# A rounded copy traced ahead of the squares, a tile in another pool, and another pacing of background loads, in a one-core encoder block

## The chip, the cores and the metric

The kernel runs on one core of one Trainium2 chip. The metric is the device time of one execution in microseconds (us). The kernel before took 1969.74 us (median of 3 runs, 1966.11 to 1972.82).

## What is computed

One encoder block on a single sequence of T = 256 tokens of width D = 2048, all in fp32. Two branches read the same normalised input, are merged by gates, and a feed-forward layer follows.

```python
mod = c_act @ ada_w + ada_b                 # six vectors of 2048: shift, scale, gate (mixer), shift, scale, gate (FFN)
h = rms_norm(x, norm_mix_w) * (1 + scale_m) + shift_m
proj = h @ w_in                             # all inputs of both branches and the merge gates
...
h_a = bidirectional(mlstm_chunkwise, ...)   # branch A: 4 mLSTM heads, key width 256, value width 512
y_a = (sigmoid(a_o) * rms_norm(h_a)) @ w_branch_a
...
q_b = l2_normalize(heads(b_q, B_HEADS, B_DK)) * (B_DK ** -0.5)
k_b = l2_normalize(heads(b_k, B_HEADS, B_DK))
o_b = bidirectional(gated_delta_chunkwise, ...)  # branch B: 16 delta-rule heads of width 128
y_b = (rms_norm(o_b) * silu(b_z)) @ w_branch_b
...
x = x + gate_m * ((g_a * y_a + g_b * y_b) @ w_out)
hf = rms_norm(x, norm_ffn_w) * (1 + scale_f) + shift_f
x = x + gate_f * ((silu(gt) * up) @ w_down) # gt, up = split(hf @ w_gate_up), width 5632
```

The result is a final RMSNorm of `x`.

## The kernel before, in words

**Weight jobs.** Nearly all of PE's time goes to products with weights. A weight block of 1 MB (`raw_...`, three buffers) is loaded by SP's queue. It is split in halves: ACT writes the rounded copy `wh_...` (L207 or L176), DVE the rest `wl_...` = raw minus copy (L209 or L178), and PE multiplies `wh` by the high part of the activations, `wh` by the low part, and `wl` by the high part. A half of a block is one step of a job, and `wh` and `wl` have three buffers each. `tjob` and `fjob` are these jobs (`fjob` for operands that come out transposed). The weight of a job is in its name: `b` and `a` for the input projection of the delta branch and of the mLSTM queries and keys, `z`, `v`, `o`, `mb`, `ma` for gates and values, `yb` and `ya` for the output projections of the branches B and A, `o` again for `w_out`, then `gt`, `up` and `d` for the feed-forward layer.

**Order.** The program is traced once in the order in which Python generators yield: `fill(n)` takes n steps of the jobs in `fills`, `drive(cores, n)` alternates a step of the branch work with n steps of jobs, and `settle()` traces evictions that were put off. A scheduler of the language then lays out one queue for each engine. It starts from the traced order and moves an instruction whose inputs or buffer it expects late behind others; an instruction that is passed through `order()` keeps its place in the program's order. On the chip each engine works through its own queue in that order and waits on semaphores, so that whatever stands behind a waiting instruction on its engine waits with it. A change of buffers alone can therefore move instructions.

**Delta heads.** For each of the 16 heads `gdn_phase1` has `kq` (queries and keys, 128x512) in fp32. ACT makes the squares `sqkq` (L596), whose sums PE takes with a column of ones (`vps`, L605) for the normalisation, and the rounded copy `kqh` (L599); DVE makes the rest `kql` (L600), and PE multiplies the split parts. `sqkq`, `kqh` and `kql` have one buffer each. At the end of a pair of heads PE transposes the result into `px` (L835), ACT scales it into `obt` (L839, 128x256, two buffers in the pool `bk`), and ACT's queue stores it to the DRAM tensor `ob_d` (L840). Group g of four heads is one tensor `ob_d[g]`.

**From branch B to its output projection.** When all heads are done, `sx.close()` gives up `bk` and the pools beside it; `ml`, which holds what the mLSTM heads need (`dn`, `hs`, `o4` and others), takes that memory. Then `o_load(g)` reads `ob_d[g]` into `o4` (L1070, GpSimd's queue, two buffers), and `o_split` makes `obh` (ACT, L1074) and `obl` (DVE, L1075), the operands of the `yb` jobs. In the same stretch the first two mLSTM heads finish: `pden` (PE, L956) are the denominators, `dn` (ACT, L958) their absolute values, `ph` (PE, L972) the numerators, `hs` (L974, L975) the quotient. `pxa` (L988) are its transposes, `hah` and `hal` (L992, L993) its split.

**The eviction pool.** `evp` lies on the other side of memory and lives until `sa.close()`. `keep_f` evicts the `a` jobs through its two buffers of tag `evf` (L355 to L357, stored to `kq_d`).

**Background loads.** The vectors of `mod` need `ada_w`: 64 blocks of 1 MB in parts of 16, each loaded into `ada` (L114, SP's queue) and multiplied and summed on DVE (L122, one instruction of 128x2048). `pump()` runs once for each step of a job. It lets an `add()` through at most once in `every[0]` steps, and not before the load is three steps old; only one block is asked for at a time, from the pool `rows_p`. `held` stops the adds for a while.

Of the kernel before, what the change touches and what calls it, by code (L numbers as in the profile page):

```python
# [9 lines left out]
F32 = mybir.dt.float32  # L10
F32R = mybir.dt.float32r
AF = mybir.ActivationFunctionType
# [3 lines left out]
P = 128  # L16
T = 256
D = 2048
# [34 lines left out]
def hybrid_block(ctx: ExitStack, tc: tile.TileContext, xr, nfr, crow, pk_d, cst_d, ada2, ada4, win0, winb, wint, wba, wbb, wo, wgu, wd, out, dbg=None):  # L53
    nc = tc.nc
    V, S, G, PE = nc.vector, nc.scalar, nc.gpsimd, nc.tensor

    def pool(stack, name, bufs=1, **kw):
        return stack.enter_context(tc.tile_pool(name=name, bufs=bufs, **kw))
# [3 lines left out]
    rows_p = pool(ctx, "rows")  # L62
# [9 lines left out]
    def order(ins, yes=True):  # L72

        return tc.keep_in_program_order(ins) if yes else ins

    def gps(name):
        return g_ps.tile([P, 512], F32, tag="g", name=name)
# [27 lines left out]
        order(S.activation(row_c[:, g * 512 : (g + 1) * 512], pc_, AF.Silu))  # L105


    asked, unasked, age = [], [], [0]

    def ask():  # L110

        part, b = unasked.pop(0)
        raw = rows_p.tile([P, D], F32, tag="ada", name=f"ada{part}_{b}")
        order(nc.sync.dma_start(raw, ada4[part - 2, b]))  # L114
        asked.append((part, b, raw))
        age[0] = 0

    def add():

        part, b, raw = asked.pop(0)  # L120
        c = part * KB + b
        order(V.scalar_tensor_tensor(raw, raw, 1.0, row_c[:, :D], ALU.mult, ALU.mult, accum_out=mod[:, c : c + 1]))  # L122
        if b == KB - 1:
            c = slice(part * KB, part * KB + KB)
            V.tensor_tensor(mod[:, c], mod[:, c], pk[:, PK_ADAB + c.start : PK_ADAB + c.stop], ALU.add)
# [18 lines left out]
    count, every = [0], [0]  # L144
    owed, held = [0], [False]

    def sums(n=1):

        while n and (unasked or asked):
            if not asked:  # L150
                ask()
            add()
            n -= 1

    def pump():
        count[0] += 1
        age[0] += 1
        if every[0] and count[0] % every[0] == 0:
            owed[0] = 1
        if asked:  # L160
            if owed[0] and age[0] > 2 and not held[0]:
                owed[0] = 0
                add()
        elif unasked and every[0]:
            ask()

    def fjob(name, src, done):

        ps = acc_ps.tile([P, 512], F32, tag="acc", name=f"acc_{name}")
        o = ps[:, :T]  # L170
        raw = raw_tile([P, KB, P], f"raw_{name}")
        nc.sync.dma_start(raw, src)
        for k0 in range(0, KB, 8):
            wh = st.tile([P, 8, P], F32R, tag="wh", bufs=3, name=f"wh_{name}_{k0}")
            wl = st.tile([P, 8, P], F32R, tag="wl", bufs=3, name=f"wl_{name}_{k0}")
            S.activation(wh, raw[:, k0 : k0 + 8], AF.Copy)  # L176
            settle()
            V.tensor_tensor(wl, raw[:, k0 : k0 + 8], wh.bitcast(F32), ALU.subtract)  # L178
            for k in range(8):
                kk = k0 + k  # L180
                PE.matmul(o, wh[:, k], woven(hh[:, kk]), start=kk == 0, stop=False)  # L181
                PE.matmul(o, wh[:, k], woven(hl[:, kk]), start=False, stop=False)  # L182
                PE.matmul(o, wl[:, k], woven(hh[:, kk]), start=False, stop=kk == KB - 1)  # L183
            pump()
            if k0:
                done(o.rearrange("p (c h) -> p h c", h=2))
            yield True
# [5 lines left out]
    def tjob(name, chunks, xh, xl, done, early=0, by_token=None, steps=1, parts=((0, slice(0, 512)), (1, slice(0, 512)))):  # L193
# [28 lines left out]
        for n, (u, k0) in enumerate(todo):  # L222
            wh, wl = made.pop(0) if made else halves(u, k0)
            for k in range(2):
                kk = 4 * u + k0 + k
                for t in range(2):
                    c = slice(t * P, (t + 1) * P)
                    order(PE.matmul(ps[t], xh[:, kk, c], woven(wh[:, k]), start=kk == 0, stop=False), early and steps > 1)  # L228
                    PE.matmul(ps[t], xl[:, kk, c], woven(wh[:, k]), start=False, stop=False)  # L229
                    PE.matmul(ps[t], xh[:, kk, c], woven(wl[:, k]), start=False, stop=kk == last)  # L230
            pump()
            if k0:
                if u == len(chunks) - 1:
                    done(ps)
            yield True
            if early and steps > 1:
                if n + early < len(todo):
                    made.append(halves(*todo[n + early]))
                yield True
# [23 lines left out]
    def fill(n=1):  # L263

        while n and fills:
            if next(fills[0], None):
                n -= 1
            else:
                fills.pop(0)
# [23 lines left out]
    evp = pool(sa, "evp", side="right")  # L293
    fr = pool(sf, "fr", side="right")
# [192 lines left out]
    with ExitStack() as s0:  # L487
# [18 lines left out]
        def loads(b):  # L506
            ra = [w0.tile([P, D + 2], F32, tag="ra", bufs=5, name=f"ra{b}_{i}") for i in range(2)]
            raw = st.tile([P, N0, P], F32, tag="raw", bufs=3, name=f"raw0_{b}")
            for i in range(2):
                order(nc.sync.dma_start(ra[i], ada2[b, :, i]))  # L510
            order(nc.sync.dma_start(raw, win0[b]))
            return ra, raw
# [10 lines left out]
        ra, raw = loads(0)  # L523
# [18 lines left out]
        for b in range(KB):  # L542
            if b:
                ra, raw = loads(b)
# [23 lines left out]
    bk = pool(sx, "bk")  # L568
# [12 lines left out]
    def gdn_phase1(h):  # L581
        settle()
        kq, vf = parts.pop(h)
# [8 lines left out]
            dec[:, 1, 256:384][:, ::-1], ab[:, 0:P][:, ::-1], ident[:, ::-1], 0.0, ALU.mult, ALU.add  # L592
        )

        sq = fr.tile([P, 2, T], F32, tag="sqkq", bufs=1, name=f"sqkq{h}")
        S.activation(sq, kq, AF.Square)  # L596
        kh = fr.tile([P, 2, T], F32R, tag="kqh", bufs=1, name=f"kqh{h}")
        kl = fr.tile([P, 2, T], F32R, tag="kql", bufs=1, name=f"kql{h}")
        S.activation(kh, kq, AF.Copy)  # L599
        V.tensor_tensor(kl, kq, kh.bitcast(F32), ALU.subtract)  # L600
        vps = gps(f"vps{h}")
        for t in range(2):
            PE.transpose(vps[:, t * P : (t + 1) * P], vf[:, t * P : (t + 1) * P], ident)
# [139 lines left out]
    def gdn_phase2(g, p):  # L743
# [88 lines left out]
        for e, on in enumerate(ons):  # L832
            h, hl_ = 4 * g + 2 * p + e, 2 * p + e
            for t in range(2):
                PE.transpose(px[:, (2 * e + t) * P : (2 * e + t + 1) * P], on[:, t], ident)  # L835
        for e in range(2):
            h, hl_ = 4 * g + 2 * p + e, 2 * p + e
            obt = bk.tile([P, T], F32, tag="obt", bufs=2, name=f"obt{h}")
            S.activation(obt, px[:, e * T : (e + 1) * T], AF.Copy, scale=pk[:, PK_GNW + h : PK_GNW + h + 1])  # L839
            S.dma_start(ob_d[g][hl_], obt)  # L840
        yield
# [27 lines left out]
    def steps(*gens):  # L869

        gens = list(gens)
        while gens:
            gens = [g for g in gens if next(g, "end") != "end"]
            if gens:
                yield

    def drive(gen, n=2):
        for _ in gen:
            fill(n)
# [29 lines left out]
    def mlstm(h):  # L909
# [84 lines left out]
        yield  # L994

    heads1 = {h: gdn_phase1(h) for h in range(NH_B)}
    after = (0, 1, 2, 1, 2, 2, 2, 2, 4, 0)
    last = (0, 1, 2, 1, 2, 2, 1, 1, 3, 0)
# [21 lines left out]
    for g in range(4):  # L1020
# [3 lines left out]
        next(blocks)  # L1024
        fill(1)
        pairs = [gdn_phase2(g, p) for p in range(2)]
        if g == 3:
            settle()
# [39 lines left out]
    def o_load(g):  # L1068
        o4 = ml.tile([P, 4, T], F32, tag="o4", bufs=2, name=f"o4_{g}")
        G.dma_start(o4, ob_d[g].rearrange("h p t -> p h t"))  # L1070
        return o4
# [40 lines left out]
            yield from y_b(g)  # L1112

    o4s = [o_load(g) for g in range(2)]
    held[0] = False
    cores = steps(*first2)
    fill(1)
# [20 lines left out]
    o_split(3, o4s[3])  # L1138
    fill(2)
    drive(cores, 3)  # L1140
    drive(steps(mlstm(2), mlstm(3)), 3)
    fill(1000)
    mgh, mgl = big(bigC, F32R, "mgh"), big(bigC, F32R, "mgl")
    sm_.close()
    sr_ = ExitStack()
    sr = pool(sr_, "sr")
    gm = sr.tile([P, D], F32, name="gm")
    dgs = {}

# [31 lines left out]
    def o_job(g, front=None):  # L1181
        return tjob(f"o{g}", [wo[g, u] for u in range(4)], mgh, mgl, lambda *a: done_o(g, *a), by_token=front,
                    parts=((0, slice(0, 512)), (1, slice(0, 256)), (1, slice(256, 512))))
# [24 lines left out]
    def root():  # L1208

        order(S.activation(rs1[:, 2:3], ones1, AF.Sqrt))  # L1210
# [83 lines left out]
    for g in range(4):  # L1294
        if g == 3:
            root()
        for i, _ in enumerate(o_job(g, front_o if g == 3 else None) if g else o_first, 0 if g else 2):
            if g == 3 and i == 3:
                every[0] = owed[0] = 0
                sums(P)  # L1300
                V.scalar_tensor_tensor(
                    affn, mod[:, 4 * KB : 5 * KB], 1.0, pk[:, PK_NFFN : PK_NFFN + KB], ALU.add, ALU.mult
                )
# [78 lines left out]
    for j in range(FB // 4):  # L1382
# [4 lines left out]
        for e2 in range(2):  # L1387
            px = gps(f"pxf{j}_{e2}")
            for e in range(2):
                f = 2 * e2 + e  # L1390
                for t in range(2):
                    PE.transpose(px[:, e * T + t * P : e * T + (t + 1) * P], sg[:, t, f * P : (f + 1) * P], ident)  # L1392
            b = 4 * j + 2 * e2
# [156 lines left out]
```

## Time and profile before

| | |
|---|---|
| median of 3 runs | 1969.74 us |
| the profiled execution | 1972.23 us |
| its span in the trace | 1970.2 us |
| mean granted TensorE clock | 0.996 |
| PE busy | 1926.1 us (98%) |
| DVE busy | 1405.9 us (71%) |
| ACT busy | 1028.4 us (52%) |
| POOL busy | 116.5 us (6%) |
| moved by DMA | 485.64 MB, mean 246 GB/s |

PE, DVE, ACT and POOL are TensorE, VectorE, ScalarE and GpSimd; PEld is TensorE's weight load, and ACTq the queue of DMAs that ACT issues. The span starts with the first and ends with the last instruction in the trace; the profiled time is 2.0 us longer. In rows of the timeline the columns are the start, the duration in us, the engine, the line, the operation, output<-input and the count; in brackets stand the idle time of the engine before it and what ended it.

### The profile page before, as it was taken

To read this page: it belongs to the slowest core of one execution; us is meant where nothing else is said; L and a number is where in the kernel's file an instruction comes from. 1 tells how busy PE (TensorE), PEld (TensorE's weight loads), DVE (VectorE), ACT (ScalarE), POOL (GpSimd) and SP (SyncE) were. 2 spreads that over 40 slices of the span, in tenths; PEclk is the share of its full clock that TensorE was granted. 3 is DMA by queue.
4 is the path that set the end of the run, shared out by engine and by line. 5 is a ranking of instruction groups with operands and counts; after the bars stand their busy time and mean duration, and the time that the engine had idled before them with its cause. 6 is when DMAs were issued, how large, how long until landed. Compare 5 with 4: busy or idle time off the path is not lost. (4 is left out here: it accounts for less than half of the span.)

```text
span 1970.2 us, 27078 instructions
## 1 busy us (share of the span) xinstructions
PE 1926.1 (98%) x10418; PEld 1701.1 (86%) x10418; DVE 1405.9 (71%) x2067; ACT 1028.4 (52%) x1553; POOL 116.5 (6%) x211
## 2 busy tenths in 40 slices
PE   8999999999999999999899999999999999999998
PEld 6878889998999899889687888888888888888886
DVE  6779886888888789866577877865665665555554
ACT  3137656765776587554534444644444444444444
POOL 0001210111011101010100000200000000000000
PEclk9999999999999999999999999999999999999999
DMA  9986676667676666587786888576676665565553
GB/s 400 421 348 225 186 248 253 206 227 232 221 226 205 225 217 237 201 287 250 268 321 220 314 314 321 213 256 235 241 269 238 235 241 206 194 214 199 207 200 142
DMA packets 78962, 485.64 MB, mean 246 GB/s; under 512 B 10585, under 2 KB 15969, under 8 KB 24433
## 3 DMA queue, kind: packets, MB, share of 16 engines
q1 hardware_dynamic: 63216, 450.69, 62.9%
q0 software_dynamic: 8160, 17.88, 4.4%
q10 hardware_dynamic: 7458, 15.36, 2.0%
q8 instruction: 81, 1.33, 0.3%
q14 instruction: 47, 0.39, 0.1%
HBM read 467.07 MB, written 16.82 MB: 246 GB/s over the span
## 5 line engine op out<-in xcount | busy, mean ns | idle before, releaser
L209 DVE TENSOR_TENSOR wl_d<-raw_d,wh_d 128x1024 fp32r<-128x1024 f32 x88 | 107.7, 1225 | 105.9 <-ACT wh_d L207 105.9
L209 DVE TENSOR_TENSOR wl_up<-raw_up,wh_up 128x1024 fp32r<-128x1024 f32 x88 | 107.7, 1225 | 100.2 <-ACT wh_up L207 100.1
L209 DVE TENSOR_TENSOR wl_gt<-raw_gt,wh_gt 128x1024 fp32r<-128x1024 f32 x88 | 108.1, 1229 | 79.2 <-ACT wh_gt L207 79.2
L181 PE MATMUL acc_b<-hh,wh_b 128*128 128x256 f32 x576 | 162.9, 283 | 0.0
L183 PE MATMUL acc_b<-hh,wl_b 128*128 128x256 f32 x576 | 159.2, 277 | 0.1
L182 PE MATMUL acc_b<-hl,wh_b 128*128 128x256 f32 x576 | 159.1, 276 | 0.0
L207 ACT ACTIVATE wh_d<-raw_d 128x1024 fp32r<-128x1024 f32 x88 | 92.9, 1056 | 126.4 <-PE acc_d L229 117.6
L207 ACT ACTIVATE wh_gt<-raw_gt 128x1024 fp32r<-128x1024 f32 x88 | 92.9, 1055 | 118.6 <-PE acc_gt L229 71.1
L122 DVE SCALAR_TENSOR_TENSOR ada<-ada,crow 128x2048 f32<-128x2048 f32 x64 | 146.2, 2284 | 7.1 <-DMA ada<-ada 7.1
L207 ACT ACTIVATE wh_up<-raw_up 128x1024 fp32r<-128x1024 f32 x88 | 92.8, 1055 | 108.1 <-PE acc_up L229 77.1
L228 PE MATMUL acc_gt<-wh_gt,hfh 128*128 128x512 f32 x352 | 135.5, 385 | 0.6 <-ACT hfh L1337 0.6
L229 PE MATMUL acc_gt<-wh_gt,hfl 128*128 128x512 f32 x352 | 135.1, 384 | 0.0
L230 PE MATMUL acc_gt<-wl_gt,hfh 128*128 128x512 f32 x352 | 133.9, 380 | 0.0
L228 PE MATMUL acc_up<-wh_up,hfh 128*128 128x512 f32 x352 | 133.4, 379 | 0.0
L229 PE MATMUL acc_up<-wh_up,hfl 128*128 128x512 f32 x352 | 133.4, 379 | 0.0
L230 PE MATMUL acc_up<-wl_up,hfh 128*128 128x512 f32 x352 | 133.4, 379 | 0.0
L228 PE MATMUL acc_d<-wh_d,ffh 128*128 128x512 f32 x344 | 130.5, 379 | 0.0
L229 PE MATMUL acc_d<-wh_d,ffl 128*128 128x512 f32 x344 | 130.5, 379 | 0.0
L230 PE MATMUL acc_d<-wl_d,ffh 128*128 128x512 f32 x344 | 130.4, 379 | 0.0
L555 PE MATMUL first<-x,raw 128*128 128x256 f32 x512 | 114.5, 382 | 6.6 <-ACT x L549 6.2
L555 PEld LDWEIGHTS first<-x,raw 128*128 128x128 f32 x512 | 96.0, 190 | 25.0 <-ACT x L549 11.9
L181 PEld LDWEIGHTS acc_b<-hh,wh_b 128*128 128x128 f32 x576 | 111.4, 193 | 0.1
(383 smaller groups left out, 5257.8 us busy)
## 6 DMA issues: line engine op xcount, KB each, us to landing
ada<-ada SPq DMA_DIRECT2D x64, 1024.0 KB, 6.2
raw_gt<-wgu SPq DMA_DIRECT2D x44, 1024.0 KB, 4.9
raw_up<-wgu SPq DMA_DIRECT2D x44, 1024.0 KB, 4.9
raw_d<-wd SPq DMA_DIRECT2D x44, 1024.0 KB, 4.9
raw_b<-winb SPq DMA_DIRECT2D x36, 1024.0 KB, 5.6
ra<-ada SPq DMA_DIRECT2D x32, 1025.0 KB, 15.7
raw<-win SPq DMA_DIRECT2D x16, 1024.0 KB, 14.5
raw_z<-wint SPq DMA_DIRECT2D x16, 1024.0 KB, 5.2
```

What stands on the lines that cost most here:

```text
L122: order(V.scalar_tensor_tensor(raw, raw, 1.0, row_c[:, :D], ALU.mult, ALU.mult, accum_out=mod[:, c : c + 1]))
L181: PE.matmul(o, wh[:, k], woven(hh[:, kk]), start=kk == 0, stop=False)
L182: PE.matmul(o, wh[:, k], woven(hl[:, kk]), start=False, stop=False)
L183: PE.matmul(o, wl[:, k], woven(hh[:, kk]), start=False, stop=kk == KB - 1)
L207: order(S.activation(wh, raws[u][:, k0 : k0 + 2], AF.Copy), early)
L209: order(V.tensor_tensor(wl, raws[u][:, k0 : k0 + 2], wh.bitcast(F32), ALU.subtract), early)
L228: order(PE.matmul(ps[t], xh[:, kk, c], woven(wh[:, k]), start=kk == 0, stop=False), early and steps > 1)
L229: PE.matmul(ps[t], xl[:, kk, c], woven(wh[:, k]), start=False, stop=False)
L230: PE.matmul(ps[t], xh[:, kk, c], woven(wl[:, k]), start=False, stop=kk == last)
L555: PE.matmul(first[o], raw[:, o], x[:, b], start=b == 0 and o % 2 == 0, stop=b == KB - 1 and o % 2 == 1)
```

## The change

It has three parts.

1. In `gdn_phase1` the rounded copy `kqh` and the rest `kql` are traced ahead of the squares `sqkq`.
2. The tile `obt` is taken from `evp` under the tag `evf`, instead of from `bk` under a tag of its own. The two buffers are then shared with the evictions of the `a` jobs.
3. The pacing of the `ada` loads. A list `homes` holds the buffers that are free to be loaded into: one in `rows_p`, and from the opening of the pool `sr` on, ahead of the `ya` jobs, a second one there. Each load carries its own age, and a load is asked for in the same `pump()` as an add, from the home that was free before it. `every[0]` is set to 0 after the first two `o_load`s, to 1 ahead of the third and fourth mLSTM heads, and to 3 when `sr` has opened. In the last `o` job, `sr`'s home is taken out again.

```diff
-    asked, unasked, age = [], [], [0]
+    asked, unasked, homes = [], [], [rows_p]
...
-        raw = rows_p.tile([P, D], F32, tag="ada", name=f"ada{part}_{b}")
+        home = homes.pop(0)
+        raw = home.tile([P, D], F32, tag="ada", name=f"ada{part}_{b}")
         order(nc.sync.dma_start(raw, ada4[part - 2, b]))
-        asked.append((part, b, raw))
-        age[0] = 0
+        asked.append([part, b, raw, home, 0])
...
-        part, b, raw = asked.pop(0)
+        part, b, raw, home, _ = asked.pop(0)
+        homes.append(home)
...
     def pump():
         count[0] += 1
-        age[0] += 1
+        for a in asked:
+            a[-1] += 1
         if every[0] and count[0] % every[0] == 0:
             owed[0] = 1
-        if asked:
-            if owed[0] and age[0] > 2 and not held[0]:
-                owed[0] = 0
-                add()
-        elif unasked and every[0]:
+        more = bool(unasked and every[0] and homes)
+        if asked and owed[0] and asked[0][-1] > 2 and not held[0]:
+            owed[0] = 0
+            add()
+        if more:
             ask()
...
-        sq = fr.tile([P, 2, T], F32, tag="sqkq", bufs=1, name=f"sqkq{h}")
-        S.activation(sq, kq, AF.Square)
         kh = fr.tile([P, 2, T], F32R, tag="kqh", bufs=1, name=f"kqh{h}")
         kl = fr.tile([P, 2, T], F32R, tag="kql", bufs=1, name=f"kql{h}")
         S.activation(kh, kq, AF.Copy)
         V.tensor_tensor(kl, kq, kh.bitcast(F32), ALU.subtract)
+        sq = fr.tile([P, 2, T], F32, tag="sqkq", bufs=1, name=f"sqkq{h}")
+        S.activation(sq, kq, AF.Square)
...
-            obt = bk.tile([P, T], F32, tag="obt", bufs=2, name=f"obt{h}")
+            obt = evp.tile([P, T], F32, tag="evf", bufs=2, name=f"obt{h}")
...
     o4s = [o_load(g) for g in range(2)]
+    every[0] = owed[0] = 0
     held[0] = False
...
     drive(cores, 3)
+    every[0] = 1
     drive(steps(mlstm(2), mlstm(3)), 3)
...
     sr = pool(sr_, "sr")
+    homes.append(sr)
+    every[0] = 3
...
                 every[0] = owed[0] = 0
                 sums(P)
+                homes.remove(sr)
```

The lines shift by 1 to 7: L207 becomes L209, L839 L841, L958 L960, L1074 L1076.

ACT's queue at the handover from branch B to the `yb` jobs, before. `obt_9347` and `obt_9350` are the last two heads' results, `dn_9382` and `dn_9399` the denominators of the first two mLSTM heads, `wh_yb_1_0` the rounded copy of the second weight block of the first `yb` job; a wait on DMAHW or DMASW is one on a DMA's landing.

```order
L349 ACTIVATE ev_ma_9339<-acc_ma_1_9137 128x512 [waits PE_49]
L839 ACTIVATE obt_9347<-px_1_9257,pk 128x256 [waits PE_49]
L350 DMA ma_d_115<-ev_ma_9339 128x1024 [waits Activation_49]
L840 DMA ob_d_123<-obt_9347 128x256 [waits DMAHW7_49,Activation_49]
L839 ACTIVATE obt_9350<-px_1_9257,pk 128x256
L207 ACTIVATE wh_yb_1_0_9510<-raw_yb_1_9508 128x1024 [waits DMAHW2_49]
L840 DMA ob_d_123<-obt_9350 128x256 [waits Activation_49]
L958 ACTIVATE dn_9382<-pden_9375 128x4 [waits DMASW5_49,DMASW6_49,DMASW4_49,DMAHW0_49,DMASW3_49,DMAHW7_49,DVE_49,PE_49]
L958 ACTIVATE dn_9399<-pden_9392 128x4 [waits PE_49]
L974 ACTIVATE hs_9387<-ph_0_0_9411,dn_9382 128x512 [waits DVE_49,PE_49]
```

The same place now:

```order
L841 ACTIVATE obt_9347<-px_1_9257,pk 128x256 [waits DMAHW4_49,PE_49]
L352 DMA ma_d_115<-ev_ma_9339 128x1024 [waits DMAHW5_49,Activation_49]
L842 DMA ob_d_123<-obt_9347 128x256 [waits DMAHW7_49,Activation_49]
L841 ACTIVATE obt_9350<-px_1_9257,pk 128x256
L960 ACTIVATE dn_9382<-pden_9375 128x4 [waits DMASW4_49,DMASW5_49,DMASW3_49,DMASW6_49,DVE_49,PE_49]
L960 ACTIVATE dn_9399<-pden_9392 128x4 [waits PE_49]
L842 DMA ob_d_123<-obt_9350 128x256 [waits DMAHW1_49,Activation_49]
L1076 ACTIVATE obh<-o_0_9369 128x1024 [waits DMASW3_49]
L976 ACTIVATE hs_9387<-ph_0_0_9411,dn_9382 128x512 [waits DVE_49,PE_49]
L209 ACTIVATE wh_yb_1_0_9508<-raw_yb_1_9506 128x1024 [waits DMAHW2_49]
```

The waits DMAHW7 and DMAHW0 at the first `dn` are gone (the landings of the two stores of `obt`, whose memory `dn` took over), `dn` stands ahead of the second store, and `obh` of group 0 stands ahead of `hs` instead of three instructions behind it. The first `obt` has a new wait (DMAHW4, the landing of an earlier store of an `a` job's eviction).

DVE's queue in the first `yb` job, before. `obl` from `o_2` and `o_3` are the low parts of groups 2 and 3, `ada_8` a background add, `wl_yb_u_k` the low part of half k of weight block u.

```order
L1075 TENSOR_TENSOR obl<-o_2_9409,obh 128x1024 [waits DMASW7_49,Activation_49]
L209 TENSOR_TENSOR wl_yb_1_2_9529<-raw_yb_1_9508,wh_yb_1_2_9528 128x1024 [waits PE_49,Activation_49]
L1075 TENSOR_TENSOR obl<-o_3_9429,obh 128x1024 [waits DMASW0_49,Activation_49]
L122 SCALAR_TENSOR_TENSOR ada_8_9490,mod<-ada_8_9490,crow 128x2048 [waits DMAHW4_49]
L209 TENSOR_TENSOR wl_yb_2_0_9548<-raw_yb_2_9545,wh_yb_2_0_9547 128x1024 [waits DMAHW3_49,PE_49,Activation_49]
```

The same place now:

```order
L1077 TENSOR_TENSOR obl<-o_2_9409,obh 128x1024 [waits DMASW7_49,Activation_49]
L1077 TENSOR_TENSOR obl<-o_3_9429,obh 128x1024 [waits DMASW0_49,Activation_49]
L211 TENSOR_TENSOR wl_yb_1_2_9527<-raw_yb_1_9506,wh_yb_1_2_9526 128x1024 [waits PE_49,Activation_49]
L211 TENSOR_TENSOR wl_yb_2_0_9545<-raw_yb_2_9542,wh_yb_2_0_9544 128x1024 [waits DMAHW3_49,PE_49,Activation_49]
L981 RECIPROCAL ssh_9406<-ssh_9406 128x2 [waits Activation_49]
```

The add of `ada_8` has left this place (and that of `ada_9`, which stood between the first and the second `yb` job); `ada_8` now stands ahead of the last half of the second `yb` job. `wl_yb_1_2` has moved behind `obl` of group 3. From the `ya` jobs on the adds stand every third step; before, every fourth. PE's queue has the same order but for some 20 instructions, and GpSimd's is unchanged.

In a delta head ACT's queue shows the first part of the change. Before, for the fifth head:

```order
L335 ACTIVATE kq_2481<-cv_1_2566 128x256 [waits DVE_49]
L596 ACTIVATE sqkq_2739<-kq_2481 128x512 [waits Activation_49]
L327 ACTIVATE pad_144<-acc_b_2_2583 128x256 [waits PE_49]
L599 ACTIVATE kqh_2741<-kq_2481 128x512
L330 ACTIVATE cv_2_2647<-pad_144,pk 128x256 [waits Activation_49]
```

And now:

```order
L337 ACTIVATE kq_2481<-cv_1_2566 128x256 [waits DVE_49]
L599 ACTIVATE kqh_2739<-kq_2481 128x512 [waits Activation_49]
L329 ACTIVATE pad_144<-acc_b_2_2583 128x256 [waits PE_49]
L602 ACTIVATE sqkq_2743<-kq_2481 128x512
L332 ACTIVATE cv_2_2647<-pad_144,pk 128x256 [waits Activation_49]
```

The two have changed places, with one eviction of a weight job (`pad`) between them; in the second and the fourth head the squares stay in front, where `kqh` has to wait for its single buffer.

## The prediction, made before the changed kernel was run

> **What bounds the kernel now.** The page's first part comes first.
>
> ```profile
> PE 1926.1 (98%) x10418; PEld 1701.1 (86%) x10418; DVE 1405.9 (71%) x2067; ACT 1028.4 (52%) x1553; POOL 116.5 (6%) x211
> ```
>
> PE sets the time: of 1970.2 us it is idle for 44, and none of its matmuls is removed here. So the change is worth what it takes from PE's waits or adds to them. The windows view tells where it waits.
>
> ```profile
> 0.00:150.00 150.00, 138.75 (x602) 113.90 (x603) 103.53 (x124) 42.09 (x78) 2.26 (x10) 1.00 0.95 385
> ...
> 955.00:1010.00 55.00, 46.48 (x200) 34.70 (x201) 36.83 (x50) 27.14 (x43) 9.33 (x15) 1.00 0.89 321
> ...
> 1080.00:1165.00 85.00, 85.00 (x408) 74.61 (x407) 71.34 (x75) 39.80 (x42) 0.00 (x0) 1.00 0.82 305
> ```
>
> The columns are the length, PE's busy time, then PEld, DVE, ACT and POOL, the granted clock, the DMA engines' busy share and GB/s. Between 955 and 1010 us, the handover to the `yb` jobs, PE idles 8.5 of 55 us; in the `ya` stage (1080 to 1165) it idles for nothing. The waits view of PE for 955:1010 names three rows, which sum to 8.5 us:
>
> ```profile
> PE acc_yb L230 <- DVE wl_yb L209: 3.5, 3, 1.6
> PE ph L972 <- ACT dn L958: 2.7, 1, 2.7
> PE pxa L988 <- DVE hal L993: 2.3, 1, 2.3
> ```
>
> All three lie where the second and third part of the change act. The timelines of the engines show why each arises.
>
> **The tile `obt` in another pool: the wait at `dn`.** The first two rows are ACT's, then two of PE's; the last row is from the view of `obt`'s tile.
>
> ```profile
> 955.66 0.33 ACTq L840 DMA_DIRECT2D ob_d<-obt  x1
> 961.69 0.24 ACT L958 ACTIVATE dn<-pden 128x4 f32<-128x4 f32 x2 [5.12 <-DMA ob_d<-obt]
> 956.40 2.82 PE L972 MATMUL ph<-vt,mdec 128*128 128x512 f32 x6
> 961.92 7.99 PE L972 MATMUL ph<-vt,mdec 128*128 128x512 f32 x18 [2.70 <-ACT dn L958]
> DMA to landing us min/median/max: 1.8/3.0/6.5
> ```
>
> `dn` takes over the memory of `obt`, so it waits until the last store of `obt` has landed, about 6 us after its issue; PE's next `ph` needs the bank that `dn` empties, and PE idles 2.70 us. With `obt` in the other pool this wait is gone from `dn`. Next in line for PE is `hs`, which in ACT's new order stands behind `obh` of group 0, and that on the load of `o_0`:
>
> ```profile
> 953.37 0.60 PE L835 MATMUL px<-cst,on 128*128 128x128 f32 x4
> 962.21 1.51 POOL L1070 DMA_DIRECT2D o<-ob_d  x2 [61.30 <-ACT dn L958]
> 967.79 1.06 ACT L1074 ACTIVATE obh<-o 128x1024 fp32r<-128x1024 f32 x1 [3.10 <-DMA o<-ob_d]
> 970.16 0.19 PEld L229 LDWEIGHTS acc_yb<-wh_yb,obl 128*128 128x128 f32 x1 [0.65 <-DVE obl L1075]
> DMA to landing us min/median/max: 4.5/5.3/6.3
> ```
>
> The last row is the view of line 1070. The load of `o_0` waited for the same stores of `obt`, and is free of them now: its memory is free after the `px` transposes of the first row, at 954.0. It lands 5.3 us later, at 959.3; `obh` takes 1.06 and `hs`, half its size, an estimated 0.7, so `hs` is out at about 961.1. PE runs through twelve `ph` passes of 0.44 (7.99 / 18) from 956.40 to 961.7 before it needs that bank. So the whole 2.70 us goes, with half a microsecond to spare; if the load takes its longest, 6.3, half a microsecond of wait is left. `obl` of group 0 is done by 963, ahead of the first `yb` matmul at 967: the 0.65 us of the fourth row goes too. **Gain 2.7 + 0.6 = 3.3.**
>
> The Trainium skill speaks against the 2.7 (DMA: Bandwidth & Descriptors, "Anatomy of one DMA"): a transfer costs about 2.0 us fixed plus its bytes at 436 GB/s. By that, a 128 KB store lands in an estimated 2.3 us, `dn` would have been in time, and the gain here would be near 0; the page adds that a landing in HBM can be surprisingly late, and the measured wait decides.
>
> **The first `yb` job: three waits for `wl`.** Rows of ACT, DVE and PE:
>
> ```profile
> 976.46 1.04 ACT L207 ACTIVATE wh_yb<-raw_yb 128x1024 fp32r<-128x1024 f32 x1
> 977.41 1.04 ACT L1074 ACTIVATE obh<-o 128x1024 fp32r<-128x1024 f32 x1
> 977.73 1.22 DVE L209 TENSOR_TENSOR wl_yb<-raw_yb,wh_yb 128x1024 fp32r<-128x1024 f32 x1
> 980.00 2.28 DVE L122 SCALAR_TENSOR_TENSOR ada<-ada,crow 128x2048 f32<-128x2048 f32 x1
> 982.21 1.22 DVE L209 TENSOR_TENSOR wl_yb<-raw_yb,wh_yb 128x1024 fp32r<-128x1024 f32 x1
> 979.00 0.48 PE L230 MATMUL acc_yb<-wl_yb,obh 128*128 128x512 f32 x1 [0.59 <-DVE wl_yb L209]
> 983.48 0.48 PE L230 MATMUL acc_yb<-wl_yb,obh 128*128 128x512 f32 x1 [1.62 <-DVE wl_yb L209]
> ```
>
> The fifth half block waits 1.62 us because DVE did an add of 2.28 us ahead of its `wl`. That add has left this place. The fourth waits 0.59 since its split stood between the two late `o` loads, and this gets no better: it now stands behind `obh` of `o_3`. `o_3` takes the buffer of `o_1`; ACT has five instructions between `hs` and `obh` of `o_1`, so that I put `obl` of `o_1` at 967.6 (an estimate). `o_3` is issued then, lands 5.3 later at 972.9, `obh`, `wh` and `wl` follow (1.06 + 1.04 + 1.22) at about 976.4, while PE, which starts the job at 967.0 (956.40 + 24 x 0.44) and takes 2.6 us a half, wants `wl` at about 975.2. I put the fourth half's wait at 1.2 us, 0.6 more than before. **Gain 1.6 - 0.6 = 1.0**; between 0 (`o_3` a microsecond later) and 2.2 (both waits gone).
>
> **The second `yb` job: an add that waits for its load.**
>
> ```profile
> 992.77 2.29 DVE L122 SCALAR_TENSOR_TENSOR ada<-ada,crow 128x2048 f32<-128x2048 f32 x1 [4.55 <-DMA ada<-ada]
> 999.59 2.87 DVE L993 SCALAR_TENSOR_TENSOR hal<-pxa,pk,hah 128x256 fp32r<-128x256 f32 x7
> 996.77 1.55 ACT L992 ACTIVATE hah<-pxa,pk 128x256 fp32r<-128x256 f32 x4
> 996.27 0.48 PE L230 MATMUL acc_yb<-wl_yb,obh 128*128 128x512 f32 x1 [1.28 <-DVE wl_yb L209]
> 1000.13 0.44 PE L988 MATMUL pxa<-cst,hs 128*128 128x128 f32 x2 [2.30 <-DVE hal L993]
> ```
>
> DVE stood for 4.55 us on the load of the next add and then added for 2.29; queued behind it were the `wl` that PE waits 1.28 us for and the `hal` that `pxa` waits 2.30 for. With neither load nor add in this stretch, `wl` is in time (1.3 gone). `hal` then follows `hah`, which ACT starts at 996.77 behind a weight copy; four of them would let `hal` end about 1.7 us earlier, and some 0.6 us of the wait stay. **Gain 1.3 + 1.7 = 3.0**; 1.3 if `hah` is no earlier at all, 3.6 if ACT's copy moves up too.
>
> **The heads.** The waits view has one row for the squares, and head 4's timeline the distance:
>
> ```profile
> PE vps L605 <- ACT sqkq L596: 0.3, 1, 0.3
> 340.04 0.62 ACT L599 ACTIVATE kqh<-kq 128x512 fp32r<-128x512 f32 x1
> 345.19 0.95 PE L605 MATMUL vps<-ones,sqkq 128*128 128x1 f32 x8
> ```
>
> Squares in the place of `kqh` end at 340.66, 4.5 us ahead of the sums that need them; no wait on `kqh` or `kql` is among PE's. The 0.3 us may grow by one activation (0.62) or go. **0**, from -0.3 to +0.6. What hides it is PE's weight jobs between; without them each of the 16 heads would pay 0.6.
>
> **What it costs.** `obt` now waits for the landing of an eviction's store in the shared buffers (view of line 357, and ACT at one of these places):
>
> ```profile
> DMA to landing us min/median/max: 1.7/4.1/7.7
> 740.52 0.84 ACT L839 ACTIVATE obt<-px,pk 128x256 f32<-128x256 f32 x2 [0.41 <-PE px L835]
> ```
>
> Where an `a` job's store is issued a step before, ACT stands 1 to 3 us by the 4.1, an estimated four times in all; the weight copies behind it are a step (2.6 us) ahead of PE. **Cost 0.3**, between 0 and 4 (1 us each). The denser adds in `ya` and `o`: 408 matmuls in 85 us are 17 blocks of 24, so a block takes 5.0 us and a step 2.5. An add of 2.28 us every 7.5 us in place of every 10 takes DVE from 71.34 of 85 us (84%) to about 91%. **Cost 0.5**, from 0 to the rival below.
>
> A last term is the clock. The windows view of 1029:1034:
>
> ```profile
> 1029.00:1034.00 5.00, 5.00 (x17) 4.10 (x16) 2.60 (x6) 1.02 (x2) 0.00 (x0) 0.66 0.78 261
> ```
>
> A granted clock of 0.66 over 5 us is 3.4 us at half speed, which costs PE 1.7 us; it comes behind a burst of one-column matmuls. Such a spell may come or go when the work ahead of it moves by microseconds: 0, +-1.7. The Trainium skill (TensorE: Matmul & The Clock Gate, "What's actually happening") has a free-running window of 3413 ns, which fits the length; by its rule the halving follows an idle window, and here PE had just been busy.
>
> **Sum:** 3.3 + 1.0 + 3.0 - 0.3 - 0.5 = 6.5 us less. The profiled execution took 1972.23 us (its span 1970.2), 2.5 over the median of the runs; 1972.23 would become 1965.7, and by the same step the median of 1969.74 becomes **1963.2 us**.
>
> **The rivals.**
>
> *All of it goes.* If `hah` moves up and the fourth half's split is in time, the three rows fall from 8.5 to nothing, and with `obl`'s 0.65 and a clock spell less the gain is 9 to 11: about 1960. For it: nothing but loads sets these times, and two 1 MB loads leave a stretch where the DMA engines are 0.89 busy. Against: the `o_3` chain above.
>
> *Another wait takes the place of `dn`'s.* The store's landing at 6.5 us is the longest of 16, the median is 3.0. If it was short in the timed runs, the 2.7 was never there; or the `o_0` load is late, and `hs` behind `obh` holds PE in its place. Either way 3.3 goes and 3 to 4 is left: about 1966.5.
>
> *Slower: the loads crowd out the weights.* From the `ya` jobs on, a load of 1 MB comes every 7.5 us in place of every 10: the 305 GB/s would become about 340. These rows are landings of 1 MB:
>
> ```profile
> raw<-win SPq DMA_DIRECT2D x16, 1024.0 KB, 14.5
> raw_ya<-wba SPq DMA_DIRECT2D x16, 1024.0 KB, 5.6
> ```
>
> The first is from the opening stage, at 385 GB/s and a share of 0.95. A block is consumed in 5.0 us and has three buffers, so the weights keep up while (landing + 5.0) / 3 is below 5.0: up to a landing of 10 us. At 14.5 each block takes 6.5 us, 1.5 more; over 11 of the 32 blocks of `ya` and `o` that is +16, net about +10: 1979. For it: DVE is nearly full there too, so that a late block can't be caught up. Against: 340 GB/s lies nearer to 305 than to 385 only by a little, but 5.6 us is far from 10.
>
> *It does nothing:* another wait follows each. 1969.7.
>
> **How the numbers follow.** Chances: forecast 0.42, all of it 0.21, another wait 0.20, crowding 0.14, nothing 0.03. About 0.3% (5.9 us) is what can be told from no change: faster lies below 1963.8. The forecast is spread by some 2.5 us and gives 0.26 faster and 0.16 same; faster is then 0.26 + 0.21 = 0.47, same 0.16 + 0.20 + 0.03 = 0.39, slower 0.14. The range holds 8 in 10 with all but crowding and the end of "all of it": 1957.5 to 1970.5.
>
> **What would show it.** Right: no wait of `ph` for `dn`, `o_0` issued by 955, no add between the `o_3` split and the end of the first `yb` job, 0.5 to 2 us left at the fourth half and at `pxa`, and PE idle under 4 us in 955:1010. Wrong: PE waits for `raw` or `wl` in 1080:1255, landings of `raw_ya` near 10 us, waits for `wh` behind `obt`, or `ph` waiting for `hs`.

## The result and the profile after

The changed kernel took 1968.9 us (median of 22 runs, 1965.65 to 1972.47), the kernel before 1972.49 in 22 runs. The ratio is 0.9983, with a 95% interval of 0.9977 to 0.9989: 3.4 us faster (2.2 to 4.5), where 6.5 were forecast. By the bound of 0.3% that is no change, though the interval excludes 1. Of the distance between 1963.2 and 1968.9, 2.75 us is the kernel before itself, whose median of 1969.74 in 3 runs became 1972.49 in 22.

The profiled execution has a span of 1966.6 us, 3.6 less, with the same mean clock of 0.996. First the windows view, in stretches that were shown of before and one ahead of them:

```profile
740.00:955.00 215.00, 208.95 (x1369) 192.68 (x1368) 159.94 (x281) 124.26 (x229) 19.16 (x36) 0.99 0.67 233
955.00:1010.00 55.00, 51.06 (x226) 39.35 (x226) 32.75 (x48) 30.08 (x47) 9.35 (x15) 0.97 0.82 295
...
1080.00:1165.00 85.00, 85.00 (x408) 74.61 (x407) 75.50 (x79) 39.69 (x41) 0.00 (x0) 1.00 0.91 345
```

PE's idle time at the handover fell from 8.5 to 3.9 us. Between 740 and 955 us it rose to 6.0 us; before it was 2.1:

```profile
740.00:955.00 215.00, 212.87 (x1421) 197.27 (x1419) 164.05 (x292) 127.96 (x235) 20.04 (x37) 1.00 0.70 242
```

In the `ya` stage PE still idles for nothing. The waits view of PE after, for 700:950 (first two rows) and 950:1010 (its only row):

```profile
PE p L791 <- DVE pt L780: 3.9, 2, 2.5
PE acc_ma L232 <- DVE wl_ma L211: 1.2, 1, 1.2
...
PE ph L974 <- ACT hs L976: 3.9, 1, 3.9
```

Two new rows of 3.9 us stand there: `pt` in two places, and `hs`. `p` and `pt` belong to the inversion of the triangular matrices of a group of heads, a chain of small matmuls and copies that runs beside the weight jobs. All three waits that the prediction had started from (3.5, 2.7, 2.3) are gone, and so is `obl`'s 0.65.

An estimate adds up the gaps between PE's successive matmuls beyond their usual spacing, by stretches, after minus before: up to 700 us -2.8, 700 to 950 us +6.0, 950 to 1050 us -5.7, the rest -0.7; -3.2 of the span's 3.6. What is taken for the usual spacing moves a figure by up to half a microsecond. A half-clock spell (some 3.4 us in which the granted clock is 0.50), worth 1.7 us, near 381 us is no longer there, and one near 922 us is new; without them the first two are -1.1 and +4.3. In the third stretch there is one before (1030 us) and one after (970 us).

**The new wait at the handover.** Timelines of the changed kernel: SP, ACT's DMAs, GpSimd, ACT, PE; the last two rows are the windows view and the landings in the view of line 1072.

```profile
955.71 0.33 SPq L206 DMA_DIRECT2D raw_yb<-wbb  x1
956.59 0.80 SPq L1081 DMA_DIRECT2D gtb<-mb_d  x2
956.85 0.36 ACTq L352 DMA_DIRECT2D ma_d<-ev_ma  x1
957.31 0.60 ACTq L842 DMA_DIRECT2D ob_d<-obt  x1
957.05 1.51 POOL L1072 DMA_DIRECT2D o<-ob_d  x2 [58.69 <-ACT ev_ma L351]
958.56 1.09 POOL L947 DMA_DIRECT2D sgo<-o_d  x2
966.60 1.06 ACT L1076 ACTIVATE obh<-o 128x1024 fp32r<-128x1024 f32 x1 [7.30 <-DMA o<-ob_d]
967.57 0.67 ACT L976 ACTIVATE hs<-ph,dn 128x512 f32<-128x512 f32 x1
968.29 7.02 PE L974 MATMUL ph<-vt,mdec 128*128 128x512 f32 x12 [3.94 <-ACT hs L976]
957.00:967.00 10.00, 7.34 (x31) 4.12 (x30) 0.68 (x6) 1.29 (x5) 2.59 (x4) 1.00 0.93 350
DMA to landing us min/median/max: 4.3/7.0/10.8
```

The load of `o_0` is free early, as forecast: it is issued right behind the `px` transposes. But seven loads and three stores are issued within 4 us, the DMA engines are busy for 0.93 of the next 10 us, and ACT gets `o_0` 9.5 us after its issue, not 5.3. ACT stands idle for 7.30 us with `hs` queued behind `obh`, and PE waits 3.94 us for the bank that `hs` empties.

Most of this company is not new. Before, too, the load of `o_0` (at 962.21) was issued between the two `gtb` and the two `sgo`, and it was with ACT after 5.6 us. What is new is that the weight block of 1 MB and the stores are still on their way. Before:

```profile
953.16 0.33 SPq L204 DMA_DIRECT2D raw_yb<-wbb  x1
954.30 0.33 ACTq L350 DMA_DIRECT2D ma_d<-ev_ma  x1
961.72 0.81 SPq L1079 DMA_DIRECT2D gtb<-mb_d  x2
963.72 1.08 POOL L945 DMA_DIRECT2D sgo<-o_d  x2
```

The block, the store of `ma_d` and the first store of `obt` had landed 6.4 to 6.5 us after their issue, by 961.2: the load of `o_0` waited for the stores of `obt`, and so met none of them. An estimate from the sizes gives the order of it: what was issued up to `o_0`, with `o_0` itself, is now 3.1 MB (`raw_yb`, two `gtb`, `ma_d`), 9.0 us at the 348 GB/s of 957.0 to 966.6; before it was 1.6 MB, 5.1 us at the 310 GB/s of 961.7 to 967.8.

**The new waits at the inversions.** ACT, DVE and PE of the changed kernel:

```profile
908.79 0.47 ACT L841 ACTIVATE obt<-px,pk 128x256 f32<-128x256 f32 x1 [1.88 <-DMA kq_d<-ev_a]
...
914.52 0.38 ACT L358 ACTIVATE ev_a<-acc_a 128x256 f32<-128x256 f32 x1 [3.72 <-DMA ob_d<-obt]
...
918.46 1.23 DVE L180 TENSOR_TENSOR wl_a<-raw_a,wh_a 128x1024 fp32r<-128x1024 f32 x1 [6.40 <-ACT wh_a L178]
919.61 2.29 DVE L123 SCALAR_TENSOR_TENSOR ada<-ada,crow 128x2048 f32<-128x2048 f32 x1
...
921.82 0.68 DVE L780 TENSOR_TENSOR pt<-p,cst 128x512 f32<-128x512 f32 x1
922.56 1.10 PE L791 MATMUL p<-X,pt 128*128 128x64 f32 x8 [2.45 <-DVE pt L780]
```

The two shared buffers make ACT wait in both directions: `obt` for the landing of an eviction's store (1.88), and the next eviction for the landing of the store of `obt` (3.72). The weight copy `wh_a` behind it comes late, DVE stands 6.40 us for it and then has a split, an add and `pt` in a row, and PE waits 2.45 us for `pt`. Near 754 us PE waits another 1.47 us for `pt`, some 13 us after `obt` stood 2.06 us for an eviction's store.

### The profile page after: what moved, and what is told of

Same layout as the page of the kernel before. It is cut to its first block, busy times and chain, and to the rows that moved or that the text cites. A ratio compares the mean times of both kernels' runs of the same rounds, so it can differ in the third digit from the quotient of the medians.

```text
span 1966.6 us, 27097 instructions
## 1 busy us (share of the span) xinstructions
PE 1925.2 (98%) x10418; PEld 1701.1 (86%) x10418; DVE 1406.0 (71%) x2067; ACT 1028.7 (52%) x1553; POOL 116.5 (6%) x211
## 5 line engine op out<-in xcount | busy, mean ns | idle before, releaser
L209 ACT ACTIVATE wh_d<-raw_d 128x1024 fp32r<-128x1024 f32 x88 | 92.9, 1056 | 126.4 <-PE acc_d L231 117.6
L209 ACT ACTIVATE wh_gt<-raw_gt 128x1024 fp32r<-128x1024 f32 x88 | 92.9, 1055 | 118.6 <-PE acc_gt L231 71.1
L209 ACT ACTIVATE wh_up<-raw_up 128x1024 fp32r<-128x1024 f32 x88 | 92.7, 1055 | 108.1 <-PE acc_up L231 77.1
L184 PEld LDWEIGHTS acc_b<-hl,wh_b 128*128 128x128 f32 x576 | 110.6, 192 | 0.1
```

What stands on the lines that cost most here:

```text
L209: order(S.activation(wh, raws[u][:, k0 : k0 + 2], AF.Copy), early)
```

## The experiments

Each was timed in 5 rounds against the kernel before on the same chip. Of every ratio the 95% interval is given; us are the ratio's share of 1972.

**The three parts alone.** The first:

```diff
 before, with only:
-        sq = ...; S.activation(sq, kq, AF.Square)
         kh = ...; kl = ...; S.activation(kh, kq, AF.Copy); V.tensor_tensor(kl, ...)
+        sq = ...; S.activation(sq, kq, AF.Square)
```

> Only the first part: the rounded copy ahead of the squares, everything else as before. Theory (the lost time comes from the shared eviction buffers): no difference, within 0.6 us of before, and no wait of p for pt at the inversions (L789 to L791). Rival (the reordered heads push DVE back, so that the pt of the inversions comes late): 3 to 4 us slower than before, with waits of p for pt of 1.5 and 2.5 us near 752 and 920 us.

0.9993 (0.9984 to 1.0002): no difference that can be told, and PE's waits view has no row of L789 for `pt`. The rival is out.

```diff
 before, with only:
-            obt = bk.tile([P, T], F32, tag="obt", bufs=2, name=f"obt{h}")
+            obt = evp.tile([P, T], F32, tag="evf", bufs=2, name=f"obt{h}")
```

> Only the second part: obt in the eviction pool, two buffers shared. Theory: ACT stands for the landing of the evictions' stores, 5 us in all, and PE waits some 4 us for pt at the inversions; at the handover dn's 2.7 and obl's 0.65 go and a wait of ph for hs of up to 4 comes; in sum 3 to 5 us slower than before. As the prediction had it: 3 us faster. Rival (the heads cause the waits for pt): no such waits here, 0 to 3 us faster.

1.0011 (1.0001 to 1.0020): 2.2 us slower (0.2 to 3.9), in the direction of the theory though smaller than its 3 to 5. The waits view of PE for 700:1010 has both new waits, at their new size:

```profile
PE ph L972 <- ACT hs L974: 4.1, 1, 4.1
PE p L789 <- DVE pt L778: 3.8, 2, 2.5
...
PE pxa L988 <- DVE hal L993: 0.7, 1, 0.7
PE acc_yb L230 <- DVE wl_yb L209: 0.5, 1, 0.5
```

The theory had left out the last two rows: with the old pacing the waits at `wl_yb` and `pxa` shrank too (from 3.5 and 2.3), as I read it because PE, held up by `hs`, came later to them.

```diff
 after, with the heads' order and obt as before: only the lists, pump(),
 every[0] = 0 / 1 / 3 and the second home
```

> Only the third part: the other pacing of the background loads, obt in its old place. Theory: the waits for wl_yb (3.5) and pxa (2.3) go, dn's 2.7 stays: 5 to 6.5 us faster than before, more than the whole change gave. Rival (the denser loads cost in ya and o what the pause gains): 0 to 2 us faster, with waits for wl or raw between 1080 and 1255 us.

0.9969 (0.9959 to 0.9980): 6.1 us faster (3.9 to 8.1), more than the whole change. PE's waits at the handover:

```profile
PE pxa L990 <- DVE hal L995: 1.4, 1, 1.4
PE acc_yb L231 <- DVE obl L1077: 0.8, 1, 0.8
PE acc_yb L232 <- DVE wl_yb L211: 0.6, 1, 0.6
PE ph L974 <- ACT dn L960: 0.6, 1, 0.6
```

From 8.5 to 3.4 us without touching `obt`. One miss: `dn`'s wait was to stay at 2.7 and was 0.6. In this execution a half-clock spell lay on the `ph` matmuls just ahead of it (granted clock 0.50 in 958:960): the six took 4.52 us in place of 2.82, so that PE came later. That part of the wait was not gained, PE spent it at work.

**Three shared buffers.**

```diff
 after, with:
-            ev = evp.tile([P, T], F32, tag="evf", bufs=2, name=f"ev_{name}")
+            ev = evp.tile([P, T], F32, tag="evf", bufs=3, name=f"ev_{name}")
 and the same for obt
```

> The whole change, but with three shared buffers instead of two, so that obt waits for a store that has long landed. Theory: no waits of ACT for kq_d stores, none of p for pt; some 4 us faster than the changed kernel, 7 to 8 us faster than before; the wait of ph for hs stays. Rival (the shared buffers have nothing to do with it): as the changed kernel, 3 to 4 us faster than before.

0.9973 (0.9964 to 0.9983): 5.3 us faster than before (3.4 to 7.1), some 2 more than the changed kernel; 4 were expected, and the two intervals overlap. The mechanism is clear from the trace. ACT at the place shown above, and the first row of PE's waits for 700:950:

```profile
906.16 0.82 ACT L841 ACTIVATE obt<-px,pk 128x256 f32<-128x256 f32 x2
910.17 0.37 ACT L358 ACTIVATE ev_a<-acc_a 128x256 f32<-128x256 f32 x1
PE acc_ma L232 <- DVE wl_ma L211: 0.6, 1, 0.6
```

Neither waits for a store any more, and no wait for `pt` is left in this stretch. The wait of `ph` for `hs` stays, at 3.9 us.

**`hs` ahead of `obh`.**

```diff
 after, with:
-            S.activation(hs[:, t], pn[0], AF.Copy, scale=dn[:, t, 0:1])
+            order(S.activation(hs[:, t], pn[0], AF.Copy, scale=dn[:, t, 0:1]), h < 2)
...
     for g in range(2):
+        if not g:
+            next(cores)
         o_split(g, o4s[g])
         o4s.append(o_load(g + 2))
-        next(cores)
+        if g:
+            next(cores)
```

> The whole change, but ACT's queue has hs of both first mLSTM heads ahead of obh of group 0. Theory (hs stands behind obh, and obh on the late load of o_0): the wait of ph for hs, 3.9 us, goes, and since ph alone keeps PE busy until obl is there, nothing takes its place; 3.5 to 4 us faster than the changed kernel, 7 to 8 faster than before. Rival (PE waits for the late load anyway, now at the first yb matmul): a wait of 2 us or more for obh or obl, at most 1.5 us faster than the changed kernel.

0.9969 (0.9957 to 0.9981): 6.1 us faster than before (3.7 to 8.5). ACT, then PE's waits for 950:1010:

```profile
958.34 0.69 ACT L976 ACTIVATE hs<-ph,dn 128x512 f32<-128x512 f32 x1 [0.79 <-PE ph L974]
...
964.76 1.06 ACT L1076 ACTIVATE obh<-o 128x1024 fp32r<-128x1024 f32 x1 [0.56 <-DMA o<-ob_d]
PE acc_yb L230 <- ACT wh_yb L209: 1.9, 1, 1.9
PE acc_yb L232 <- DVE wl_yb L211: 0.7, 1, 0.7
```

`ph` no longer waits, with the load nearly as late (9.5 us to `obh`): what cost the 3.9 us was the place of `hs` in ACT's queue behind a load. But 2.6 came back as waits for the fourth half block, the one that the prediction had put at 1.2 us. PE's idle time at the handover fell by 1.3 only, from 3.9 to 2.6. In time it is 2.7 us ahead of the changed kernel, between the theory (3.5 to 4) and the rival (at most 1.5), but the intervals of the two kernels overlap, so the time decides for neither. What came back did so for another reason than the rival's, a split and not `obh` or `obl`.

**Two loads less in the crowd.**

```diff
 after, y_b(g) for g < 2:
-        nc.sync.dma_start(gt, mb_d[g])
+        for i, x in enumerate(tjob(...)):
+            if i == 4:
+                order(S.dma_start(gt, mb_d[g]))
+            yield x
```

> The whole change, but the first two gate loads gtb (512 KB each, SP's queue, issued half a microsecond ahead of the load of o_0) are issued some 25 us later. Theory (o_0 lands 9.4 us after its issue because all loads that were freed together share the DMA engines): the load of o_0 lands 2 to 3 us earlier, the wait of ph for hs falls from 3.9 to 1 to 2 us, 2 to 3 us faster than the changed kernel. Rival (the load is late for a reason of its own, its queue or its wait for the store): still 9 to 10 us to landing, the wait unchanged, the time as the changed kernel's.

0.9976 (0.9966 to 0.9987), 4.7 us faster than before and not told apart from the changed kernel in time. GpSimd, ACT, and PE's waits:

```profile
955.92 1.51 POOL L1072 DMA_DIRECT2D o<-ob_d  x2 [56.78 <-ACT ev_ma L351]
963.76 1.06 ACT L1076 ACTIVATE obh<-o 128x1024 fp32r<-128x1024 f32 x1 [5.60 <-DMA o<-ob_d]
PE ph L974 <- ACT hs L976: 2.2, 1, 2.2
PE acc_yb L232 <- DVE wl_yb L211: 0.8, 1, 0.8
PE pxa L990 <- DVE hal L995: 0.5, 1, 0.5
```

From issue to `obh` it is 7.8 us in place of 9.5, and PE's wait for `hs` falls from 3.9 to 2.2: company makes the landing late. Of the 2 to 3 us by which the load was to land earlier, 1.7 came. The gain in time is not shown: 1.3 us came back as waits of `wl_yb` and `pxa`, and PE's idle time at the handover fell by 0.5 only, to 3.5. The 7.8 us are still 2.2 above the 5.6 of before (the estimate from the sizes gives 6.3 here, so it is a rough one). That the weight block and the stores make up this rest is argued from the issues, no run moved them alone; but with `obt` alone moved the load took 9.7 us to `obh`, and with the pacing alone 6.4.

**Both repairs.**

> Both repairs: three shared buffers and hs ahead of obh. Theory (two separate costs): they add up, 9 to 10 us faster than before, PE idle under 1 us between 955 and 1010 us and no wait of p for pt. Rival (the two overlap, since a PE that comes later finds the load landed): 6 to 7 us faster than before.

0.9954 (0.9942 to 0.9967): 9.1 us faster than before (6.5 to 11.4). The rival's 6 to 7 lie at the edge of that interval, but the trace has neither the wait for `pt` nor the one for `hs`. The two costs add up, as far as the times tell, and PE's idle time at the handover is 2.0 us:

```profile
955.00:1010.00 55.00, 53.01 (x228) 41.20 (x228) 39.01 (x54) 29.82 (x43) 7.84 (x14) 1.00 0.87 319
PE acc_yb L230 <- ACT wh_yb L209: 1.2, 1, 1.2
```

I had expected under 1. What is left is again the fourth half block.

**The pause without the denser pace.**

```diff
 the pacing alone, with:
-    homes.append(sr)
-    every[0] = 3
+    every[0] = 4
...
-                homes.remove(sr)
```

> The pacing alone and of it only the pause at the handover: one home, an add every fourth step in ya and o as before, the last blocks of the part loaded in a row in the last o job; heads and obt as before. Theory (the pause gives the gain and the denser pace only makes up for its missed adds): the waits for wl_yb and pxa go as with the whole pacing, and the last blocks that are left over cost 5 to 15 us in the last o job, PE waiting for wl_o behind adds that wait for their loads. Rival (the pause alone does it all): 5 to 6.5 us faster than before, as with the whole pacing.

1.0042 (1.0029 to 1.0054): 8.3 us slower than before. The handover is as good as with the whole pacing; the price comes 250 us later. PE's waits for 1080:1270, and DVE's last add:

```profile
PE acc_gt L230 <- ACT hfh L1342: 9.8, 1, 9.8
PE pxn L1328 <- ACT xn L1266: 3.6, 1, 3.6
...
1262.15 2.32 DVE L123 SCALAR_TENSOR_TENSOR ada<-ada,crow 128x2048 f32<-128x2048 f32 x1 [5.01 <-DMA ada<-ada]
```

The last blocks come one after the other at the end of the last `o` job, the last add stands 5.01 us for its load, and the scale of the feed-forward layer needs them all. Behind the wait of 9.8 us PE starts at half clock besides (granted clock 0.68 over 1266:1274, an estimated 2.6 us more). The size was expected, the place not: PE waits for `hfh` behind the job, not for `wl_o` in it.

**A version faster than both.** Both repairs, and the split of the fourth half block of the first `yb` job ahead of `obh` of groups 2 and 3:

```diff
-            order(S.activation(wh, raws[u][:, k0 : k0 + 2], AF.Copy), early)
+            order(S.activation(wh, raws[u][:, k0 : k0 + 2], AF.Copy), early or (name, u, k0) == ("yb0", 1, 2))
 (wl likewise)
...
-    o_split(2, o4s[2])
     fill(1000)
...
-    fill(3)
-    o_split(3, o4s[3])
-    fill(2)
+    fill(4)
+    o_split(2, o4s[2])
+    fill(1)
+    o_split(3, o4s[3])
```

> Three shared buffers and hs ahead of obh, and besides the split of the fourth half block of the first yb job ahead of obh of groups 2 and 3 on ACT and DVE. Theory (what is left at the handover is that split, 1.2 and 0.7 us, behind the late o loads): both waits go, PE idle under 0.5 us between 955 and 1010 us, 1.5 to 2 us faster than with the two repairs alone, 10.5 to 11.5 faster than before. Rival (the loads of o_2 and o_3 are needed just as late): a wait of PE for obh or obl of 1 us or more in place of these, 9 us faster than before as with the two repairs.

1959.61 us, 0.9940 (0.9927 to 0.9952): 11.8 us faster than before (9.5 to 14.4). PE at the handover:

```profile
955.00:1010.00 55.00, 54.65 (x240) 43.28 (x240) 40.59 (x60) 29.51 (x43) 8.20 (x14) 1.00 0.90 335
PE pxa L990 <- DVE hal L995: 0.3, 1, 0.3
```

0.35 us of idle time is left of 8.5. The same with the squares in front again:

> The same with the squares ahead of the rounded copy again, as before. Theory (the order in the heads is worth nothing): as the other kernel of this call within 1 us. Rival (the order in the heads gives 1 to 2 us, as the first part alone seemed to): 1 to 2 us slower than the other.

0.9945 (0.9931 to 0.9958) against 0.9940: the order in the heads is worth nothing that these runs can tell. Here and with the first part alone the new order came out ahead, by 1.0 and 1.4 us, both within the noise.

## Where the prediction failed, and where it held

The change gave 3.4 us where 6.5 were forecast. Two terms of the sum failed, the one on `dn` and `o_0` and the one on the shared buffers.

**The pause at the handover: right.** The two steps on the `yb` jobs were put at 1.0 + 3.0 us. With the pacing alone, where `hs` holds nothing up, the rows they came from fell from 5.8 us to 2.0 (1.4 at `pxa`, 0.6 at `wl_yb`), a gain of 3.8. In the whole change they fell to nothing, but there PE came 3.9 us late, and that alone, with the old pacing, had left only 1.2 of them. The same lateness hid the fourth half block's split, which was to cost 0.6 us more; where PE is in time (`hs` ahead of `obh`) it waits 1.9 and 0.7 there. The sub-step was right in its mechanism, and with 2.6 us for the 1.2 it was sized too small.

**`dn` and `o_0`: the wait changed its place.** The step that failed is "it lands 5.3 us later, at 959.3". The 5.3 us were the median of four landings in the kernel before. There `o_0` was issued only after the stores of `obt` had landed, and by then the weight block had landed too; the wait that the change takes away was also what kept the load out of their company. Set free at 957, it went with all of them. The prediction named the order of ACT (`hs` behind `obh` behind the load) and bounded the wait by the longest landing seen, 6.3; it was 9.5 to `obh`, and so "half a microsecond of wait" was 3.9. Instead of 3.3 us gained there was a loss of about 0.6 (2.7 and 0.65 gone, 3.9 new). This was the rival "another wait takes the place of `dn`'s". That the time also came out at about its price (3 to 4 us left of 6.5) is in part luck, since the 4 us at the shared buffers were not in it. The rule of the Trainium skill that was set against the trace (DMA: Bandwidth & Descriptors, "Anatomy of one DMA"), a fit for DMAs that GpSimd issues, as it does this load though not the store of `obt`, gives an estimated 3.2 us for such a load of 512 KB. It has no term for other transfers, and the trace does not agree: it was 5.6 us before, 9.5 here, and 7.8 with two loads fewer.

**The shared buffers: sized wrong.** The term "Cost 0.3", between 0 and 4, measured 4.3 in PE's waits (3.9 for `pt`, 0.4 for `X`, a tile of the same inversions that ACT writes). Two things were missing. Only `obt` waiting for evictions was counted, not the next eviction waiting for `obt`, 3.72 us of ACT. And the cover that was named, weight copies a step ahead of PE, holds for weight jobs; the inversion's `pt` stands on DVE behind the late splits and an add and has no such lead. Three buffers take all of it away.

**The denser pace in `ya` and `o`: right.** 340 GB/s were expected and 345 measured, DVE at 91% and measured at 89% (75.50 of 85). PE waits for nothing there. Landings of `raw_ya` rose from 5.6 to 7.1 us, under the 10 from which the rival would have decided:

```profile
raw_ya<-wba SPq DMA_DIRECT2D x16, 1024.0 KB, 7.1
```

The pause alone shows that the pace is no extra: without it the pause loses 8.3 us.

**The heads: right** at nothing, as far as can be told. **The clock: right** at nothing in sum, with spells at other places.

What stays open: the sum of the parts alone (-1.4, +2.2, -6.1) is -5.3, and the whole gave -3.4. The intervals of the three, about 2 us to each side, allow for that, and an overlap goes the same way: of the 5.8 us of waits at `wl_yb` and `pxa` the pacing alone takes 3.8 and the lateness that the move of `obt` brings takes 4.6, so that 2.6 are counted twice. On the other side PE's waits do not account for all of the gain: the 5.8 us of the pause's rows less 0.6 and 4.3 are 0.9. Part of the rest lies, in the two profiled executions, in stretches for which the prediction had no term (about 1.1 us up to 700 us); no run here says what causes it.

## What to carry to other kernels

When a change takes a wait away, list what the freed transfer will now meet: everything else that the same event had held back, and everything that had landed during the wait. Price the transfer as one of that crowd, not by its landing in the old trace. When two users share a ring of buffers, price the wait in both directions, and look for the chain behind it that has the least lead, not for the one that is easiest to see. In an in-order queue an instruction behind a load is the place to look first: moving `hs` ahead of `obh` took all 3.9 us of its wait away, thinning out the company of the load 1.7.

## What the runs showed of the hardware

At a DMA share of 0.93 and 350 GB/s, a load of 512 KB was usable 9.5 us after its issue, where it took 5.6 before, with five of the same loads beside it but a 1 MB load and the stores already landed; taking two loads of 512 KB out of the company gave 1.7 us back. Over 85 us, 345 GB/s at a share of 0.91 held without a wait of PE. Half-clock spells fell at other places with shifts of a few microseconds: at 381 and 1030 us before, at 922 and 970 after, besides one near 1255 in both. With the pacing alone one lay right behind `pden`, a burst of one-column matmuls, with PE busy (0.50 in 957:960); behind a wait of 9.8 us (the pause alone) PE started at half clock (0.50 in 1266:1271).
